# Moving both operands of the large matmuls to equal offsets, and norming two token tiles at a time, in a hybrid encoder layer on one core

## The chip, the core and the metric

The kernel runs on one core of a Trainium2 chip. A core has five engines that each take their instructions in order: TensorE (PE in the profile: matmuls and transposes; its weight loads stand as PEld), VectorE (DVE), ScalarE (ACT), GpSimd (POOL) and SyncE (SP, which issues most loads). They wait for one another through semaphores. Operands lie in SBUF, products in the eight banks of PSUM. The metric is the time of one execution on the device in microseconds; less is better.

## The reference

One layer over 512 tokens of width 2048 in float32: four token mixers that share one input projection, cross-attention to 256 memory tokens, and a gated feed-forward network. Each of the three has a norm before it and one behind it.

```python
def rmsnorm(x, g):
    xf = x.astype(jnp.float32)
    y = xf * lax.rsqrt(jnp.mean(xf * xf, axis=-1, keepdims=True) + EPS)
    return (y * g.astype(jnp.float32)).astype(x.dtype)

def swiglu_ffn(h, w_gu, w_down):
    gate, up = jnp.split(h @ w_gu, 2, axis=-1)
    return (jax.nn.silu(gate) * up) @ w_down

def reference(x, mem, norm_g, w_in, ...):
        u = rmsnorm(x, g[MIX_PRE]) @ w_in[l]
        u_a, u_b, u_c, u_d = jnp.split(u, IN_SPLITS, axis=-1)
        mixed = jnp.concatenate([
            short_conv_mixer(u_a, ...), multiscale_pool_mixer(u_b, ...),
            gated_deltanet_mixer(u_c, ...), mamba2_mixer(u_d, ...)], axis=-1)
        x = x + rmsnorm(mixed @ w_out[l], g[MIX_POST])
        xa = memory_cross_attention(rmsnorm(x, g[XA_PRE]), rmsnorm(mem, g[MEM_NORM]), ...)
        x = x + rmsnorm(xa, g[XA_POST])
        x = x + rmsnorm(swiglu_ffn(rmsnorm(x, g[FFN_PRE]), w_gu, w_down), g[FFN_POST])
```

`ffn_w_gu` is 2048 by 11264 and `ffn_w_down` 5632 by 2048.

## The kernel before

**Products.** TensorE multiplies in a reduced float format (fp32r), so each float32 operand is split into a high and a low part: ACT casts the high part (L149, L152, L962), VectorE subtracts it to get the low one (L150, L153, L963). `mul3` (L167 to L170) makes one product of three matmuls: high by high (L168), high by low (L169), low by high (L170). The first operand that a row names behind the arrow is the moving one, the second the one whose 128 columns are loaded.

**Large projections.** `proj_a` and `proj_b` run over pieces of a weight matrix of 256 by 512 (1,024 numbers a partition); each piece is loaded on SP, split into `whi` and `wlo`, and multiplied with all token tiles: matmuls of 512 columns. The pool `wp` has three buffers of each. `act` holds the activations of a stage, eight buffers; `pt` holds the attention's probabilities, `at_v` the values, for `value_out` (L871). The pools are laid out one behind the other in SBUF; a small pool `padp` on the right and a tile `pad` in `gp` shift what follows.

**Stages.** K projection (to about 115 us), input projection with the gated delta rule and the other mixers (to 750), V projection (to 1000), output projection with the first norm (`advance`), `value_out`, query projection and attention (to 1325), attention's output projection `y_proj` with `vw_d` (1325 to 1421), the second norm, gate and up projection (1478 to 2367), down projection (2375 to 2762), last step.

**The second norm.** `phase2` hands `y_proj` a list of steps (L921): column block 0 for all four token tiles, blocks 1 to 3 for tiles 0 and 1, then blocks 1 to 3 for tiles 2 and 3. After block 3 of a pair, `then` calls `advance_t` (L925) for it. For one tile after the other it loads the residual `x1_d`, forms the reciprocal root of the mean square (`mean_rsqrt`, twelve small instructions on VectorE), adds (L938), stores `x2_d`, norms again (squares on ACT, a second chain), scales on ACT (L941), transposes on TensorE (L946, sixteen) and evicts on VectorE (L948) into `xT`. For tiles 0 and 1 the factors L1 and L2 are split at once. Before the norm of tiles 2 and 3, `begin` (L1051) starts blocks 0 and 1 of the next stage.

**Gate and up projection.** 44 blocks; each computes a 2-by-2 block product with seven products in place of eight (the Winograd form of Strassen's scheme). Product m multiplies the left factor Lm (from `xT`, made once by `left_parts`, L965) with a right factor made from four weight quarters (`right_parts`, L988); it is 24 matmuls of 256 columns. `ORDER` (L959) is the order of the products. Products 1 and 2 go to their own half banks A and B; `gate_first` (L1041) copies A on ACT, adds B on VectorE and forms the gate. Product 6 adds to A, 5 and 3 to Cc, 7 and 4 to A. ACT copies 6 to `f_y` (L1087) before product 7 may write A again.

**Down projection.** Ten panels with the same seven products, 512 columns each, factors B1 to B7 from the hidden activations; `panel` (L1145) loads the four quarters B11, B12, B21, B22 in this order, 1 MB each, and splits them with `factor` (L1171).

**What sets the order.** The code is written per stage; a scheduler moves independent instructions past one another before the program is fixed, so that, for instance, 11 matmuls of product 3 stand ahead of product 7. [...]

Of the kernel before, what the change touches and what calls it, by code (L numbers as in the profile page):

```python
# [7 lines left out]
F32 = mybir.dt.float32  # L8
# [53 lines left out]
def build(tc, x, mem, norm_g, w_in, conv_a_w, pool_w, pool_scale, gdn_conv_w, gdn_A_log,  # L62
# [13 lines left out]
    es_act, es_ps, es_wp, es_stg, es_early = (ExitStack() for _ in range(5))  # L76
    wp = pool("wp", 3, stack=es_wp)

    pool("padp", side="right").tile([P, 8], F32, name="pad")
# [647 lines left out]
    def y_proj(act, W, g, yp, steps):  # L727
# [5 lines left out]
        ss = yp.tile([P, NT, 4], F32, name="yss")  # L733
# [29 lines left out]
    def phase1():  # L763
# [16 lines left out]
        with s1:  # L780
            with ExitStack() as s2:
# [6 lines left out]
                gp.tile([P, 8], F32, name="pad")  # L788
# [97 lines left out]
    def phase2(act):  # L886
        with ExitStack() as s0:
# [22 lines left out]
            def then(i):  # L910
                def f(y, ss):
                    if i == 1:
                        for j in range(2):
                            begun[j] = begin(j, L, ep)
                    advance_t((2 * i, 2 * i + 1), y, ss, xT, pl2)
                    if i == 0:
                        for sub in range(2):
                            split3(L[1][sub], xT[0][0][sub])
                            split3(L[2][sub], xT[1][0][sub])
                return f  # L920
# [4 lines left out]
    def advance_t(tiles, y, ss, xT, pl):  # L925


        for t in tiles:
            rows = slice(t * P, (t + 1) * P)
            xt = pl.tile([P, D], F32, name="ad_x", bufs=2)  # L930
            nc.sync.dma_start(xt, x1_d[rows])
            s = sm.tile([P, 1], F32, name="rs_s")
            nc.vector.tensor_reduce(s, ss[:, t], axis=AX.X, op=ALU.add)
            r = sm.tile([P, 1], F32, name="rs_r")
            mean_rsqrt(r, s, 1, D)
            for q in range(4):
                qs = slice(q * 512, (q + 1) * 512)
                nc.vector.scalar_tensor_tensor(xt[:, qs], y[:, t, qs], r, xt[:, qs], op0=ALU.mult, op1=ALU.add)  # L938
            nc.gpsimd.dma_start(x2_d[rows], xt)
            n = norm_rows(xt, pl)  # L940
            nc.scalar.activation(xt, xt, AF.Copy, scale=n)  # L941
            for q in range(4):
                tp = ps.tile([P, 4, P], F32, name="ps")
                for j in range(4):
                    k = q * 4 + j
                    nc.tensor.transpose(tp[:, j], xt[:, k * P:(k + 1) * P], ident)  # L946
# [12 lines left out]
    ORDER = (1, 2, 5, 6, 7, 3, 4)  # L959
# [5 lines left out]
    def left_parts(A11, A12, A21, A22, tmp, L, given=()):  # L965
# [3 lines left out]
        for m, a in ((1, A11), (2, A12)):  # L969
# [18 lines left out]
    def right_parts(B11, B12, B21, B22, new, begun=False):  # L988

        tt = nc.vector.tensor_tensor  # L990
        if not begun:
            yield B11
            yield B21
# [11 lines left out]
    def gate_up(xT, L, begun):  # L1005

        with ExitStack() as s0:
# [14 lines left out]
            tp = pool("tp", 2, "right", s0, reuse_waits="tile")  # L1022
            for j in range(HT):
# [14 lines left out]
    def half_bank():  # L1038
        return mm.tile([P, 512], F32, name="mm")[:, 0:256]

    def gate_first(A, B, pl):  # L1041

        g, th = pl.tile([P, 256], F32, name="f_g"), pl.tile([P, 256], F32, name="f_t")
        X = pl.tile([P, 256], F32, name="f_x", bufs=1)
        nc.scalar.copy(X, A)
        nc.vector.tensor_tensor(g, B, X, op=ALU.add)
        nc.scalar.activation(th, g, AF.Tanh, scale=0.5)
        nc.vector.scalar_tensor_tensor(g, th, 1.0, g, op0=ALU.add, op1=ALU.mult)
        return g

    def begin(j, L, pl):  # L1051

        A, B = half_bank(), half_bank()
        for m, bank in ((1, A), (2, B)):
            b = wp.tile([P, 8, P], F32, name="raw")
            nc.sync.dma_start(b, w_gu[j, m - 1, 0])
            product(bank, split_w(b), L, m)
        return A, gate_first(A, B, pl)

    def block(j, L, rp, tp, begun):  # L1060
# [7 lines left out]
        parts = right_parts(*q, lambda: tp.tile([P, 8, P], F32, name="sum"), bool(begun))  # L1068
        if begun:
            A, g = begun  # L1070
        else:
            A, B = half_bank(), half_bank()
            for m, bank in ((1, A), (2, B)):
# [246 lines left out]
```

## Time and profile before

| | us |
|---|---|
| median of three runs | 2833.37 (2831.52 to 2834.23) |
| the profiled execution | 2830.88 |
| its span in the profile | 2829.1 |
| TensorE busy | 2736.0 |
| VectorE busy | 1863.6 |
| ACT busy | 1226.0 |
| y_proj's end to the first L5 matmul | 56.6 |
| last matmul of gate_up to the first of the down projection | 8.3 |

The profile shows one execution. Busy time counts an engine's own instructions; a matmul's end is modelled, so consecutive matmuls overlap in the rows, and the pace is read from the distance of their starts. An idle time is named with what ended it.

### The profile page before, as it was taken

How to read it: one execution, taken by the hardware profiler on the slowest of the kernel's cores; microseconds unless marked ns; L12 is line 12 of the kernel's file. 1: busy time of each engine (PE TensorE's matmuls, PEld its weight loads, DVE VectorE, ACT ScalarE, POOL GpSimd, SP SyncE). 2: the span in 40 equal slices, each digit the busy share in tenths (PEclk: the TensorE clock that was granted, in tenths of full speed). 3: DMA queues.
4: the chain of work that ended last, by engine and by line, in shares of the span. 5: the costliest groups of instructions: out<-in, count | busy, mean ns of one | idle time of the engine just before them, and what ended most of it. 6: DMA issues, size and time to landing. Idle time of an engine off the chain costs nothing. (4 is left out here: it accounts for less than half of the span.)

```text
span 2829.1 us, 39953 instructions
## 1 busy us (share of the span) xinstructions
PE 2736.0 (97%) x15890; PEld 2380.0 (84%) x15890; DVE 1863.6 (66%) x2743; ACT 1226.0 (43%) x1866; POOL 115.4 (4%) x175
## 2 busy tenths in 40 slices
PE   8999999999999999999949999999999998999997
PEld 6778788878788877888749999999999997888885
DVE  5735557455752364433787777777777778999976
ACT  5623433233552254432544444444444444555542
POOL 0000001100000001000000000000000000000002
PEclk9999999999999999999979999999999999999998
DMA  8633322334675267433633333333333335567656
GB/s 286 232 100 89 91 71 79 112 119 144 206 268 184 92 237 261 157 100 122 209 119 123 123 113 120 116 116 117 116 116 116 120 113 210 200 185 201 168 141 220
DMA packets 160725, 425.23 MB, mean 150 GB/s; under 512 B 18061, under 2 KB 29210, under 8 KB 149658
## 3 DMA queue, kind: packets, MB, share of 16 engines
q1 hardware_dynamic: 145626, 363.96, 38.9%
q0 software_dynamic: 14912, 58.73, 7.6%
q8 instruction: 124, 2.03, 0.3%
q14 instruction: 63, 0.52, 0.1%
HBM read 348.16 MB, written 74.47 MB: 149 GB/s over the span
## 5 line engine op out<-in xcount | busy, mean ns | idle before, releaser
L153 DVE SCALAR_TENSOR_TENSOR wlo<-raw,PA,whi 128x512 fp32r<-128x512 f32 x368 | 263.5, 748 | 313.5 <-ACT whi L152 313.3
L152 ACT ACTIVATE whi<-raw,PA 128x512 fp32r<-128x512 f32 x368 | 248.0, 718 | 415.2 <-PE mm L169 222.8
L168 PE MATMUL mm<-act,whi 128*128 128x512 f32 x832 | 334.4, 402 | 0.0
L170 PE MATMUL mm<-act,wlo 128*128 128x512 f32 x832 | 331.2, 398 | 0.0
L169 PE MATMUL mm<-act,whi 128*128 128x512 f32 x832 | 330.7, 398 | 0.0
L962 ACT CAST whi<-raw 128x1024 fp32r<-128x1024 f32 x176 | 184.7, 1050 | 279.6 <-PE mm L169 270.4
L963 DVE TENSOR_TENSOR wlo<-raw,whi 128x1024 fp32r<-128x1024 f32 x176 | 215.4, 1225 | 79.9 <-ACT whi L962 79.7
L168 PE MATMUL mm<-whi,act 128*128 128x512 f32 x640 | 255.0, 399 | 2.3 <-ACT act L149 2.3
L169 PE MATMUL mm<-wlo,act 128*128 128x512 f32 x640 | 254.4, 398 | 1.6 <-DVE wlo L153 1.6
L170 PE MATMUL mm<-whi,act 128*128 128x512 f32 x640 | 253.6, 397 | 0.2 <-DVE act L150 0.2
L150 DVE TENSOR_TENSOR wlo<-raw,whi 128x1024 fp32r<-128x1024 f32 x92 | 112.6, 1225 | 195.4 <-ACT whi L149 195.3
L962 ACT CAST whi<-sum 128x1024 fp32r<-128x1024 f32 x132 | 138.5, 1050 | 219.1 <-PE mm L169 211.6
L963 DVE TENSOR_TENSOR wlo<-sum,whi 128x1024 fp32r<-128x1024 f32 x132 | 161.5, 1223 | 79.4 <-ACT whi L962 79.2
L170 PEld LDWEIGHTS mm<-act,wlo 128*128 128x128 f32 x832 | 156.8, 188 | 36.2 <-issue 0.5
L169 PEld LDWEIGHTS mm<-act,whi 128*128 128x128 f32 x832 | 157.1, 189 | 35.0 <-issue 0.7
L168 PEld LDWEIGHTS mm<-act,whi 128*128 128x128 f32 x832 | 157.1, 189 | 34.9 <-issue 0.7
L149 ACT CAST whi<-raw 128x1024 fp32r<-128x1024 f32 x92 | 96.6, 1051 | 191.7 <-PE mm L170 141.1
L168 PEld LDWEIGHTS mm<-whi,act 128*128 128x128 f32 x640 | 120.9, 189 | 31.6 <-ACT act L149 4.2
L169 PEld LDWEIGHTS mm<-wlo,act 128*128 128x128 f32 x640 | 121.0, 189 | 30.1 <-DVE wlo L153 2.9
L170 PEld LDWEIGHTS mm<-whi,act 128*128 128x128 f32 x640 | 121.0, 189 | 27.9 <-DVE act L150 0.6
L168 PE MATMUL mm<-L5h,whi 128*128 128x256 f32 x352 | 100.6, 286 | 23.4 <-ACT whi L962 23.4
L962 ACT CAST whB<-rawB 128x1024 fp32r<-128x1024 f32 x80 | 83.8, 1052 | 53.0 <-PE mm L170 46.9
(539 smaller groups left out, 7262.8 us busy)
## 6 DMA issues: line engine op xcount, KB each, us to landing
raw<-in_w_gu_dram SPq DMA_DIRECT2D x180, 512.0 KB, 3.7
raw<-in_w_in_dram SPq DMA_DIRECT2D x88, 512.0 KB, 3.6
rawB<-in_w_down_dram SPq DMA_DIRECT2D x40, 1024.0 KB, 6.8
raw<-in_xa_wkv_dram SPq DMA_DIRECT2D x64, 512.0 KB, 4.7
raw<-in_w_out_dram SPq DMA_DIRECT2D x32, 512.0 KB, 3.7
raw<-in_xa_wo_dram SPq DMA_DIRECT2D x32, 512.0 KB, 6.3
raw<-in_xa_wq_dram SPq DMA_DIRECT2D x32, 512.0 KB, 3.8
raw<-vw_d SPq DMA_DIRECT2D x28, 512.0 KB, 4.4
```

Source lines behind the costliest of these rows:

```text
L149: nc.scalar.copy(hi, src)
L150: nc.vector.tensor_tensor(lo, src, hi.bitcast(F32), op=ALU.subtract)
L152: nc.scalar.activation(hi, src, AF.Copy, scale=scale)
L153: nc.vector.scalar_tensor_tensor(lo, src, scale, hi.bitcast(F32), op0=ALU.mult, op1=ALU.subtract)
L168: nc.tensor.matmul(o, ah, bh, start=start, stop=False, skip_group_check=reopen)
L169: nc.tensor.matmul(o, ah, bl, start=False, stop=False, skip_group_check=reopen)
L170: nc.tensor.matmul(o, al, bh, start=False, stop=stop, skip_group_check=reopen)
L962: nc.scalar.copy(hl[0], src)
L963: nc.vector.tensor_tensor(hl[1], src, hl[0].bitcast(F32), op=ALU.subtract)
```

## The change

It has five parts. Pads: a pool `padl` of 32 numbers on the left, `padp` of 104 in place of 8, the `pad` in `gp` of 72 in place of 8, and `yss` as a tile of 128 columns. They shift what follows, so that the weight tiles, `act`, `at_v` in both its pools, L1 and L2, B1 and B2 and the last step's tiles begin 64 bytes past a multiple of 512 bytes; before, `act`, L1, L2, B1, B2 and the last step's tiles began 448 past, `at_v` in the pool `adp` 384. Order of products: 2 before 1, with A and B in the two halves of one bank, ACT copying B; Cc moves to the pool `ps`. Second norm: `advance_t` works on its two tiles together, with one chain of small instructions for both, and scales the second tile on VectorE. Five blocks instead of two are begun before their stage. In a panel the same order, so B21 is split first.

```diff
+    pool("padl").tile([P, 32], F32, name="pad")
     wp = pool("wp", 3, stack=es_wp)
-    pool("padp", side="right").tile([P, 8], F32, name="pad")
+    pool("padp", side="right").tile([P, 104], F32, name="pad")
...
-        ss = yp.tile([P, NT, 4], F32, name="yss")
+        ss = yp.tile([P, 128], F32, name="yss")[:, 0:4 * NT].rearrange("p (t c) -> p t c", c=4)
...
-                gp.tile([P, 8], F32, name="pad")
+                gp.tile([P, 72], F32, name="pad")
...
                 def f(y, ss):
-                    if i == 1:
-                        for j in range(2):
-                            begun[j] = begin(j, L, ep)
                     advance_t((2 * i, 2 * i + 1), y, ss, xT, pl2)
                     if i == 0:
                         for sub in range(2):
                             split3(L[1][sub], xT[0][0][sub])
                             split3(L[2][sub], xT[1][0][sub])
+                    else:
+                        for j in range(3):
+                            begun[j] = begin(j, L, ep)
...
     def advance_t(tiles, y, ss, xT, pl):
+        xs = []
         for t in tiles:
             xt = pl.tile([P, D], F32, name="ad_x", bufs=2)
+            nc.sync.dma_start(xt, x1_d[t * P:(t + 1) * P])
+            xs.append(xt)
+        s = sm.tile([P, 2], F32, name="rs_s")
+        for i, t in enumerate(tiles):
+            nc.vector.tensor_reduce(s[:, i:i + 1], ss[:, t], axis=AX.X, op=ALU.add)
+        r = sm.tile([P, 2], F32, name="rs_r")
+        mean_rsqrt(r, s, 2, D)
+        sq = sm.tile([P, 2, 2], F32, name="nr_q")
+        for i, t in enumerate(tiles):
+            for hf in range(2):
+                qs = slice(hf * 1024, (hf + 1) * 1024)
+                nc.vector.scalar_tensor_tensor(xs[i][:, qs], y[:, t, qs], r[:, i:i + 1], xs[i][:, qs],
+                                               op0=ALU.mult, op1=ALU.add)
+                sumsq(xs[i][:, qs], sq[:, i, hf:hf + 1], pl)
+            nc.gpsimd.dma_start(x2_d[t * P:(t + 1) * P], xs[i])
+        s2 = sm.tile([P, 2], F32, name="nr_s2")
+        nc.vector.tensor_reduce(s2, sq, axis=AX.X, op=ALU.add)
+        n = sm.tile([P, 2], F32, name="nr_r2")
+        mean_rsqrt(n, s2, 2, D)
+        for hf in range(2):
+            qs = slice(hf * 1024, (hf + 1) * 1024)
+            nc.scalar.activation(xs[0][:, qs], xs[0][:, qs], AF.Copy, scale=n[:, 0:1])
+            nc.vector.tensor_scalar(xs[1][:, qs], xs[1][:, qs], n[:, 1:2], None, op0=ALU.mult)
+        for q in (0, 2, 1, 3):
+            for i, t in enumerate(tiles):
                 tp = ps.tile([P, 4, P], F32, name="ps")
...
-    ORDER = (1, 2, 5, 6, 7, 3, 4)
+    ORDER = (2, 1, 5, 6, 7, 3, 4)
...
-        for m, a in ((1, A11), (2, A12)):
+        for m, a in ((2, A12), (1, A11)):
...
+            yield B21
             yield B11
-            yield B21
...
+            for j in range(3, 5):
+                begun[j] = begin(j, L, tp)
             for j in range(HT):
                 block(j, L, rp, tp, begun.get(j))
...
+    def begin(j, L, pl, B11=None, B21=None):
+        bank = mm.tile([P, 512], F32, name="mm")
+        A, B = bank[:, 0:256], bank[:, 256:512]
+        tl = lambda n, bufs: pl.tile([P, 256], F32, name="f_" + n, bufs=bufs)
+        X, g = tl("x", 1), tl("g", 3)
+        for m, o, kh, b in ((2, B, 1, B21), (1, A, 0, B11)):
+            if b is None:
+                b = wp.tile([P, 8, P], F32, name="raw")
+                nc.sync.dma_start(b, w_gu[j, kh, 0])
+            product(o, split_w(b), L, m)
+            if m == 2:
+                nc.scalar.copy(X, B)
+        nc.vector.tensor_tensor(g, A, X, op=ALU.add)
+        nc.scalar.activation(X, g, AF.Tanh, scale=0.5)
+        nc.vector.scalar_tensor_tensor(g, X, 1.0, g, op0=ALU.add, op1=ALU.mult)
+        return A, g
...
-        Cc = half_bank()
+        A, g = begun or begin(j, L, tp, q[0], q[2])
+        Cc = ps.tile([P, 512], F32, name="ps")[:, 0:256]
...
-        ws = {1: factor(), 2: factor()}
+        ws = {m: factor() for m in ORDER[:2]}
...
-            if m == 1:
+            if m == 2:
                 X = new("eX")
-                copy(X, A)
-            elif m == 2:
+                copy(X, B)
+            elif m == 1:
                 for t in range(2):
-                    tt(X[:, t], B[t], X[:, t], op=ALU.add)
+                    tt(X[:, t], A[t], X[:, t], op=ALU.add)
```

How it stands on the engines, at three places. First TensorE in a block of gate_up that was not begun early, before: the end of product 2 and the start of product 5 (what a row waits for stands in brackets).

```order
L168 MATMUL mm<-L2h,whi 128x256
L169 MATMUL mm<-L2l,whi 128x256
L170 MATMUL mm<-L2h,wlo 128x256
L168 MATMUL mm<-L5h,whi 128x256 [waits Activation_49]
L169 MATMUL mm<-L5l,whi 128x256
L170 MATMUL mm<-L5h,wlo 128x256 [waits DVE_49]
L168 MATMUL mm<-L5h,whi 128x256
```

After, the same place: product 2 is through, eleven matmuls of product 5 have been started, and product 1 follows.

```order
L170 MATMUL ps<-L5l,whi 128x256
L171 MATMUL ps<-L5h,wlo 128x256
L169 MATMUL ps<-L5h,whi 128x256
L170 MATMUL ps<-L5l,whi 128x256
L169 MATMUL mm<-L1h,whi 128x256 [waits Activation_49]
L170 MATMUL mm<-L1l,whi 128x256
L171 MATMUL mm<-L1h,wlo 128x256
```

Product 1 used to stand ahead of product 2 and wait for its weights alone; now it stands among the matmuls of product 5, and its first matmul waits for an instruction of ACT.

Second, TensorE at the end of the second norm, before: the last transposes, and L5.

```order
L946 MATMUL ps<-C,ad_x 128x128 x3
L946 MATMUL ps<-C,ad_x 128x128 [waits DVE_49]
L946 MATMUL ps<-C,ad_x 128x128 x3
L168 MATMUL mm<-L5h,whi 128x256 [waits Activation_49]
L169 MATMUL mm<-L5l,whi 128x256 [waits DVE_49]
L168 MATMUL mm<-L6h,whi 128x256 [waits Activation_49]
L170 MATMUL mm<-L5h,wlo 128x256 [waits DVE_49]
```

After, the last transposes:

```order
L960 MATMUL ps<-C,ad_x 128x128 [waits DVE_49]
L960 MATMUL ps<-C,ad_x 128x128 x3
L170 MATMUL mm<-L2l,whi 128x256
L960 MATMUL ps<-C,ad_x 128x128 [waits DVE_49]
L960 MATMUL ps<-C,ad_x 128x128 x3
L169 MATMUL mm<-L1h,whi 128x256 [waits Activation_49]
L170 MATMUL mm<-L1l,whi 128x256
L171 MATMUL mm<-L1h,wlo 128x256
```

The transposes now stand between matmuls of products 2 and 1 of blocks begun early; L5 comes about 90 matmuls further on.

Third, ACT at the entry to the down projection, before (`whB` are high parts of weights, `rawB` a load, `hq` and `tmp` hidden activations):

```order
L962 CAST B5h<-tmp 128x1024 [waits DVE_49]
L962 CAST B7h<-hq 128x1024 [waits DVE_49,Activation_49]
L962 CAST whB<-rawB 128x1024 [waits DMAHW2_49]
L962 CAST whB<-rawB 128x1024 [waits DMAHW4_49]
L962 CAST B6h<-tmp 128x1024 [waits DVE_49]
L962 CAST whB<-rawB 128x1024 [waits DMAHW4_49]
L962 CAST whB<-rawB 128x1024
```

After:

```order
L976 CAST B5h<-tmp 128x1024 [waits DVE_49]
L976 CAST B7h<-hq 128x1024 [waits DVE_49,Activation_49]
L976 CAST B6h<-tmp 128x1024 [waits DVE_49]
L976 CAST B3h<-hq 128x1024 [waits DVE_49]
L976 CAST whB<-rawB 128x1024 [waits DMAHW2_49,DMASW3_49,DMASW1_49]
L976 CAST whB<-rawB 128x1024 [waits Activation_49]
L976 CAST whB<-rawB 128x1024 [waits DMAHW0_49]
```

Two more casts of left factors (B6, B3) now stand ahead of the first cast of weights, which reads another load than before.

## Rows read from the trace of the kernel before

**Rows 1.** The page's first section: busy time of each engine, its share, instructions
```profile
PE 2736.0 (97%) x15890; PEld 2380.0 (84%) x15890; DVE 1863.6 (66%) x2743; ACT 1226.0 (43%) x1866; POOL 115.4 (4%) x175
```

**Rows 2.** TensorE's waits: line, releaser, us in total, times, longest
```profile
PE mm L168 <- ACT whB L962: 8.0, 1, 8.0
```

**Rows 3.** Timeline of TensorE: start, duration, line, operands, [idle before, releaser]
```profile
1401.62 2.10 PE L946 MATMUL ps<-C,ad_x 128*128 128x128 f32 x16 [1.51 <-ACT ad_x L941]
...
1414.74 2.10 PE L946 MATMUL ps<-C,ad_x 128*128 128x128 f32 x16 [1.23 <-ACT ad_x L941]
...
1477.83 0.58 PE L168 MATMUL mm<-L5h,whi 128*128 128x256 f32 x1 [23.43 <-ACT whi L962]
```

**Rows 4.** Timeline of TensorE: ends of two dense stretches
```profile
838.29 0.39 PE L170 MATMUL mm<-whi,act 128*128 128x512 f32 x1
...
1016.31 0.40 PE L168 MATMUL mm<-whi,at_vh 128*128 128x512 f32 x1
...
1329.19 0.39 PE L168 MATMUL mm<-whi,pth 128*128 128x512 f32 x1
...
1399.72 0.39 PE L170 MATMUL mm<-whi,ptl 128*128 128x512 f32 x1
```

**Rows 5.** Groups by line, TensorE, 1086 to 1143, then 1153 to 1165
```profile
L170 PE MATMUL mm<-whi,at_vl 128*128 128x512 f32 x17 | 6.7, 395 | 0.0
...
L170 PE MATMUL mm<-whi,at_vl 128*128 128x512 f32 x18 | 7.0, 389 | 0.0
```

**Rows 6.** Stretches, matmuls reading act: length, PE busy (count), clock, DMA
```profile
0.00:100.00 100.00, 82.83 (x338) 1.00 0.89 304
300.00:560.00 260.00, 192.43 (x741) 1.00 0.29 86
...
750.00:800.00 50.00, 37.07 (x151) 1.00 0.55 173
```

**Rows 7.** Timeline of TensorE: a block, first matmuls of products 1, 5, 3
```profile
1878.45 0.28 PE L168 MATMUL mm<-L1h,whi 128*128 128x256 f32 x1
...
1884.15 0.28 PE L168 MATMUL mm<-L5h,whi 128*128 128x256 f32 x1
...
1889.90 0.28 PE L168 MATMUL mm<-L3h,whi 128*128 128x256 f32 x1
```

**Rows 8.** Timeline of ACT: the copy of product 6 in a block
```profile
1809.48 0.36 ACT L1087 COPY f_y<-mm 128x256 f32<-128x256 f32 x1
```

**Rows 9.** Timeline of TensorE behind that copy
```profile
1809.59 0.28 PE L169 MATMUL mm<-L3l,whi 128*128 128x256 f32 x1
1809.89 0.38 PE L168 MATMUL mm<-L7h,whi 128*128 128x256 f32 x1
1810.12 0.28 PE L169 MATMUL mm<-L7l,whi 128*128 128x256 f32 x1
```

**Rows 10.** Timeline of VectorE: evictions, a split, a root's chain, a gate step
```profile
1415.43 2.48 DVE L948 TENSOR_TENSOR stg<-ps,PA 128x512 f32<-128x512 f32 x4 [1.39 <-PE ps L946]
1417.84 1.22 DVE L963 TENSOR_TENSOR L1l<-stg,L1h 128x1024 fp32r<-128x1024 f32 x1
...
1427.35 0.15 DVE L228 TENSOR_SCALAR mr_v<-rs_s 128x1 f32<-128x1 f32 x1
...
1429.67 0.75 DVE L938 SCALAR_TENSOR_TENSOR ad_x<-y,rs_r,ad_x 128x512 f32<-128x512 f32 x1
...
1431.47 0.42 DVE L1046 TENSOR_TENSOR f_g<-mm,f_x 128x256 f32<-128x256 f32 x1
```

**Rows 11.** The stretch to L5: length, PE, PEld, DVE, ACT, POOL, clock
```profile
1421.20:1477.80 56.60, 19.32 (x129) 18.02 (x128) 48.20 (x98) 23.74 (x27) 1.06 (x2) 0.70 0.29 103
```

**Rows 12.** Line 309: count, duration min/median/max ns, first, last, shape
```profile
L309 DVE TENSOR_SCALAR xt<-xt,nr_r x4: 1287/1288/1291, 84.0 to 108.1; 128x2048 f32<-128x2048 f32 x4
```

**Rows 13.** Timeline of ACT: first and third load of the down projection
```profile
2374.42 1.99 ACT L962 CAST whB<-rawB 128x1024 fp32r<-128x1024 f32 x2 [1.05 <-DMA rawB<-in_w_down_dram]
...
2379.41 2.00 ACT L962 CAST whB<-rawB 128x1024 fp32r<-128x1024 f32 x2 [2.05 <-DMA rawB<-in_w_down_dram]
```

More of the change, by code (lines that the diff above doesn't have):

```diff
@@ L925, in advance_t @@
     def advance_t(tiles, y, ss, xT, pl):
+        xs = []
         for t in tiles:
-            rows = slice(t * P, (t + 1) * P)
             xt = pl.tile([P, D], F32, name="ad_x", bufs=2)
[L931 to L942, printed above, removed]
+            nc.sync.dma_start(xt, x1_d[t * P:(t + 1) * P])
[23 more added lines that the diff above has]
+            for i, t in enumerate(tiles):
                 tp = ps.tile([P, 4, P], F32, name="ps")
@@ L945, in advance_t @@
                     k = q * 4 + j
-                    nc.tensor.transpose(tp[:, j], xt[:, k * P:(k + 1) * P], ident)
+                    nc.tensor.transpose(tp[:, j], xs[i][:, k * P:(k + 1) * P], ident)
                 o = t % 2 * P
@@ L1036, in split_w @@
         return w
[L1038 to L1058, printed above, removed]
+    def begin(j, L, pl, B11=None, B21=None):
[14 more added lines that the diff above has]
+        return A, g
     def block(j, L, rp, tp, begun):
@@ L1067, in block @@
         tl = lambda n, bufs=1: tp.tile([P, 256], F32, name="f_" + n, bufs=bufs)
[L1068 to L1073, printed above, removed]
-                product(bank, split_w(next(parts)), L, m)
-            g = gate_first(A, B, tp)
-        Cc = half_bank()
+        parts = right_parts(*q, lambda: tp.tile([P, 8, P], F32, name="sum"), True)
+        A, g = begun or begin(j, L, tp, q[0], q[2])
+        Cc = ps.tile([P, 512], F32, name="ps")[:, 0:256]
         bank = {6: A, 5: Cc, 7: A, 3: Cc, 4: A}
@@ L1095, in block @@
             else:
-                th = tl("t", 2)
+                th = tl("t")
                 nc.scalar.activation(th, A, AF.Tanh, scale=0.5)
```

## The prediction

> **What bounds the kernel now.** I read the page's first section first: TensorE is busy 2736.0 of 2829.1 us [rows 1], so only two things can move the end: the pace at which TensorE takes its matmuls, and the few places where it stands. For the places I read the table of TensorE's waits. It names the first product of the down projection, 8.0 us [rows 2]; TensorE's timeline shows the transposes of the second norm waiting and the longest wait of all, 23.43 us at 1477.83, before the first product that needs the left factors [rows 3]. For the pace I read the distance of one matmul's start from the next where nothing waits: first and last start of a dense stretch, divided by the matmuls in between.
>
> The pace has two values for the same shape. From 838.29 to 1016.31 lie 766 starts of 512 columns, 232.4 ns each; from 1329.19 to 1399.72 there are 311, 226.8 ns each [rows 4]. In the built program the first stretch reads an `act` tile that begins 448 bytes past a multiple of 512 against a weight tile that begins 64 past one; the second reads `pt` and weights, both 64 past. That the operands' distance decides, and not what they hold, is borne out by one piece of code that runs at either: `value_out` takes 395 ns a matmul with `at_v` 384 past, and 389 ns where the same lines run with `at_v` 64 past [rows 5].
>
> **Part 1, the pads.** After the change both operands of all the large matmuls lie 64 past. By the program 5,376 matmuls of 512 columns go from unequal to equal: 4,416 that read `act`, 288 of `value_out`, 480 with B1 or B2 in the down projection, 192 in the last step. The two rows of spacing differ by 5.6 ns, the rows of `at_v` by 6; I take 5.7, so 5,376 x 5.7 = 30.6 us if TensorE sets the pace everywhere. It does not in the start-up, in the recurrence and around 750 to 800, where loads or other engines' chains pace it; 338 + 741 + 151 = 1,230 `act` matmuls lie there [rows 6], and I credit none of them: 4,146 x 5.7 = **-23.6 us**. Ends: -30.6 (all), and -18 if a quarter of the others is lost behind short interruptions, of which the stretches of rows 4 are free.
>
> The same step costs something at 256 columns. In one block of gate_up the 48 matmuls of products 1 and 2 (unequal) take 1878.45 to 1884.15, 118.8 ns each; the next 48 (products 5 and 6, equal) take 5.75 us, 119.8 ns [rows 7]. 44 blocks x 48 x 1.2 ns (1.0 by this block, rounded up as a median block shows 120.0) = **+2.5 us**, with 0 as the other end.
>
> **Part 2, a wait in every block.** A block now runs product 2 into the upper half of a bank, product 1 into the lower half of the same bank, and ACT copies product 2 in between. The order of after shows what this does: the first matmul of product 1 waits for ACT's copy, and eleven matmuls of product 5 stand ahead of it. Before has this very figure once a block: product 7 waits for the copy of product 6, eleven matmuls of product 3 stand ahead. There ACT's copy starts at 1809.48, takes 0.36 and ends after the eleven are through [rows 8]; TensorE goes on at 1809.89 where 1809.71 was due, and needs 0.23 for the next step where 0.12 is usual [rows 9]. That is 0.18 + 0.11 = 0.29 us. On ACT's queue the new copy stands behind one cast of weights just as that one does, and nobody else is kept. 39 of the 44 blocks run this way (five are begun early): 39 x 0.29 = **+11.3 us**. Ends: 0, if ACT happens to be free when product 2 ends; +17, if half a cast more (some 0.15 us) comes before the copy in each.
>
> By the rows alone the wait could be thought needless, since the two halves are different addresses. [...]
>
> **Part 3, tiles 0 and 1 together.** Inside the last projection the transposes of tile 0 and of tile 1 each waited, 1.51 and 1.23 us [rows 3]. Now 32 transposes come in a row behind 47 more projection matmuls, so these 2.7 us go. What comes instead: VectorE gets eight evictions of 0.62 (2.48 for four), four splits of L1 and L2 at 1.2 (1.14 start to start) and two evictions of y at 0.6, 10.8 us in a block [rows 10], and the split whose low half the next projection matmuls need stands behind it, 1.1 more. TensorE covers 4.2 us of that with the transposes (2 x 2.10, rows 3) and 1.4 with six matmuls that need no low half. New wait 11.9 - 5.6 = 6.3, less 2.7: +3.6, and with a little for ACT's casts ahead of the splits **+4 us**. Ends 0 and +9.
>
> **Part 4, tiles 2 and 3 together, five blocks begun early.** From the projection's end to the first L5 matmul 56.6 us pass, in which TensorE has 96 matmuls of blocks 0 and 1 and 32 transposes; VectorE is busy 48.2 of them, ACT 23.7 [rows 11]. So the chain on VectorE decides when L5 starts, and it has 8.4 us of slack at most. Removed: two of four reciprocal-root chains, 2.3 us each (1427.35 to 1429.67, rows 10), -4.6. Added: the scaling of tile 3, 1.3 by the row of a tensor_scalar over 2048 columns [rows 12] and 0.1 for a second instruction; six splits of weights for blocks 2 to 4 at 1.14, 6.8; six gate steps at about 0.35 start to start (0.42 each, rows 10), 2.1. Net +5.7 us of work against 8.4 of slack, so L5 starts 0 to 5.7 later; I take 3. In return the first two products of blocks 2, 3 and 4, 144 matmuls x 0.119 = 17.1 us, run while TensorE would stand. **-14 us**. Ends -18 (L5 no later, the clock kept up: its mean in the stretch is 0.70 before) and -8 (the three blocks' weights stand behind the left factors on VectorE, and TensorE, which keeps its order, waits for them before L5). Loads for three blocks are issued on SP earlier, 512 KB each, in a stretch whose DMA share is 0.29; that hides them.
>
> **Part 5, the entry to the down projection.** The first factor is now B21, the third of the 1 MB loads, since the loads keep their order. ACT began to cast the first at 2374.42 and the third at 2379.41, each when its load had landed [rows 13]; TensorE, which waited 8.0 us [rows 2], waits 5.0 longer: **+5 us**, ends +2 (the factor after it is then ready) and +6.
>
> Cost nothing: the third product bank moved to the other PSUM pool, fewer buffers for the tanh tile, the squares taken in halves on ACT (the same columns), the loads of x1 issued together.
>
> **Sum.** -23.6 + 2.5 + 11.3 + 4 - 14 + 5 = -14.8. The profiled execution took 2830.9 us, so 2816.1; the median of the runs is 2833.4, 2.5 above it, so **2819 us** (rounded).
>
> **Rivals.** *The equality does not bring the pace.* The slow pace would then belong to what `act` and `at_v` adjoin and not to their distance from the weights; part 1 drops out: -14.8 + 23.6 - 2.5 = +6.3, 2840 us, slower. The kernel turns slower at all once under a quarter of part 1 comes (6.3 of 23.6), and by over 0.2% once next to nothing does. Against it speaks `at_v` [rows 5]; for it that no row shows an `act` tile at 64. [...]
>
> *The early blocks only move the wait.* If VectorE does its queue in order, the weights of blocks 3 and 4 come after the left factors, L5 comes after those products on TensorE, and what is gained on five blocks is waited in front of them: part 4 falls from -14 to 0, giving 2833 us, no change. For it: 48.2 of 56.6 us busy on VectorE; against: at most 5.7 us of work is added there against 17.1 taken from TensorE.
>
> *All of the pace and no wait in the blocks.* If the copy is ready when the eleven matmuls end, and the 1,230 matmuls speed up too: -30.6 + 2.5 + 0 + 4 - 14 + 5 = -33, 2800 us. Against it the same figure costs 0.29 us in each block of before.
>
> **How the numbers follow.** The ends of the terms, combined as independent (root of the sum of squares), reach 15 us below the sum and 11 above; three quarters of that, 2808 to 2827, I call the forecast, 0.64; the moved wait 0.15; the pace without effect 0.08; all of the pace 0.10; the rest, 0.03, is spread. A measurement of this kernel can tell about 0.2%, 5.7 us, from no change: faster is below 2827.7, slower above 2839.1. Faster: 0.64 + 0.10 + 0.02 = 0.76; same: 0.15 + 0.01 = 0.16; slower 0.08. The range runs from 2806, between the forecast and the full gain, to 2833, at the moved wait.
>
> **What would show it.** Part 1: 227 ns between starts in the stretch that had 232.4, and 389 for `at_v` everywhere. Part 2: one more step of about 0.3 us in each block, before product 1, put down to ACT's copy. Part 3: no wait at the transposes, but one of some 6 us at a low product in the projection's last column. Part 4: L5 some 60 us after the projection's end, and blocks 2 to 4 with five products. Part 5: the first down matmul 13 us after the last of gate_up. I am wrong if the pace does not change, or if TensorE stands over 10 us longer between the projection and L5 than worked out.

## The result and the profile after

The changed kernel takes 2818.56 us (median of five runs, 2812.74 to 2820.15) against 2833.37 before: a ratio of 0.9945, 95% interval 0.993 to 0.9959, 14.8 us faster. The forecast was 2819. In the profiles the spans are 2814.2 and 2829.1, 14.9 apart, so the profile of after can be read as it stands, stage by stage.

The page's first section of after, which answers to [rows 1] (busy us, share of the span, instructions):

```profile
PE 2721.0 (97%) x15890; PEld 2384.8 (85%) x15890; DVE 1868.8 (66%) x2693; ACT 1220.6 (43%) x1874; POOL 115.9 (4%) x175
```

TensorE is busy 15 us less in a span that is 15 us shorter: the change made its matmuls faster and left the standing, taken together, about as long. Where it stands now, by the table of TensorE's waits (line, releaser, us in total, times, longest), beside [rows 2, 3]:

```profile
PE mm L171 <- DVE wlo L977: 17.6, 2, 15.2
PE mm L169 <- ACT whB L976: 13.4, 1, 13.4
PE mm L170 <- DVE wlo L151: 5.9, 5, 3.9
```

The 23.43 us before L5 became 15.2 at a low product of a block begun early; the wait for the first down factor went from 8.0 to 13.4; a new one of 3.9 came inside the attention's projection.

**The pace.** TensorE's timeline, ends of the dense stretch of the V projection, as [rows 4]:

```profile
830.39 0.39 PE L171 MATMUL mm<-whi,act 128*128 128x512 f32 x1
...
1004.06 0.39 PE L169 MATMUL mm<-whi,at_vh 128*128 128x512 f32 x1
```

766 steps in 173.67 us, 226.7 ns each, where it took 232.4. The group of `at_v` in the pool where it was unequal, in the form of [rows 5] (count, us, mean ns):

```profile
L171 PE MATMUL mm<-whi,at_vl 128*128 128x512 f32 x8 | 3.1, 390 | 0.0
```

390 ns, where 395 stood.

**A block of gate_up.** TensorE where product 1 now waits, and ACT's timeline at that place, to be read as [rows 9] and [rows 8]:

```profile
1900.60 0.28 PE L170 MATMUL ps<-L5l,whi 128*128 128x256 f32 x1
1900.85 0.38 PE L169 MATMUL mm<-L1h,whi 128*128 128x256 f32 x1
1901.08 0.28 PE L170 MATMUL mm<-L1l,whi 128*128 128x256 f32 x1
```

```profile
1899.48 1.06 ACT L976 CAST whi<-sum 128x1024 fp32r<-128x1024 f32 x1 [1.55 <-PE mm L170]
1900.43 0.37 ACT L1067 COPY f_x<-mm 128x256 f32<-128x256 f32 x1
```

The copy of product 2 (`f_x`) begins behind a cast of weights; the first matmul of product 1 comes 0.25 us after the one ahead of it and the next 0.23 later, where 0.12 is due: 0.13 + 0.10 us more, as forecast in kind.

**The norm of tiles 0 and 1.** TensorE (first the transposes, then the low product) and VectorE:

```profile
1388.71 3.61 PE L960 MATMUL ps<-C,ad_x 128*128 128x128 f32 x16 [2.01 <-ACT ad_x L953]
...
1402.57 0.79 PE L170 MATMUL mm<-wlo,pth 128*128 128x512 f32 x1 [3.92 <-DVE wlo L151]
```

```profile
1391.57 4.08 DVE L962 TENSOR_TENSOR stg<-ps,PA 128x512 f32<-128x512 f32 x6 [0.16 <-PE ps L960]
1395.57 1.22 DVE L977 TENSOR_TENSOR L1l<-stg,L1h 128x1024 fp32r<-128x1024 f32 x1
...
1401.31 3.48 DVE L151 TENSOR_TENSOR wlo<-raw,whi 128x1024 fp32r<-128x1024 f32 x3
```

The granted clock there, in the columns of [rows 6] but for all matmuls:

```profile
1388.71:1392.00 3.29, 3.29 (x16) 0.50 0.44 145
1402.57:1405.70 3.13, 3.13 (x7) 0.50 0.53 188
```

The transposes still wait, 2.01 us, and the first sixteen take 3.61 in place of 2.10 [rows 3]. TensorE had stood 0.81, 0.68 and 2.01 us from 1375.5 on, and was then granted 0.50: a transpose starts every 213 ns, where at 1.00 it takes 109. VectorE's evictions wait for the transposes (0.16 us ahead of the third), not the other way round. Behind the evictions come the four splits of L1 and L2 from 1395.57 on, and only at 1401.31 the low parts that the projection needs. After the 3.92 us of waiting for them the clock is 0.50 again, and seven matmuls take 427 ns each in place of 227.

**Tiles 2 and 3, blocks begun early.** TensorE at the low product of block 3 and at L5, and VectorE ahead of it:

```profile
1458.39 0.58 PE L171 MATMUL mm<-L2h,wlo 128*128 128x256 f32 x1 [15.16 <-DVE wlo L977]
...
1469.01 0.28 PE L169 MATMUL ps<-L5h,whi 128*128 128x256 f32 x1
```

```profile
1454.85 2.35 DVE L977 TENSOR_TENSOR L4l<-stg,L4h 128x1024 fp32r<-128x1024 f32 x2
1457.12 3.48 DVE L977 TENSOR_TENSOR wlo<-raw,whi 128x1024 fp32r<-128x1024 f32 x3
```

VectorE splits the last left factor (L4) and only then the weights of block 3. L5 follows 57.3 us after the projection's last matmul (1411.69), 56.8 before.

**Entry to the down projection.** TensorE and ACT, beside [rows 13]:

```profile
2363.62 1.22 PE L169 MATMUL mm<-whB,B2h 128*128 128x512 f32 x2 [13.40 <-ACT whB L976]
```

```profile
2359.77 1.04 ACT L976 CAST B3h<-hq 128x1024 fp32r<-128x1024 f32 x1 [0.21 <-DVE hq L996]
2362.52 3.89 ACT L976 CAST whB<-rawB 128x1024 fp32r<-128x1024 f32 x4 [1.70 <-DMA rawB<-in_w_down_dram]
```

ACT is ready at 2360.8 and stands until the third load lands. The first matmul comes 13.7 us after gate_up's last; before it was 8.3.

The stages of the two traces side by side, from matmul to matmul of the same number (a minus is a gain):

| stretch | before, us | after, us | difference | forecast |
|---|---|---|---|---|
| start to the attention's projection | 1324.8 | 1307.2 | -17.6 | -19.8 |
| inside it, the 96th low product to its end | 29.0 | 37.2 | +8.2 | +4 |
| its end to the end of the fifth block | 151.7 | 134.5 | -17.2 | -14 |
| the other 39 blocks | 794.5 | 803.7 | +9.3 | +13.5 |
| entry to the down projection, first panel | 48.8 | 54.3 | +5.5 | +4.7 |
| the other panels, the last step, the end | | | -3.2 | -3.6 |

From the first to the 96th low product of the attention's projection both take 67.2 us. The forecasts in the first and last line are part 1 split by its counts of matmuls; the fourth line has part 2 and 39 blocks' share of the 256-column loss.

### The profile page after: what moved, and what is told of

The parts are those of the page before. It is cut to its first block, busy times and chain, and to the rows that moved or that the text cites. A ratio compares the mean times of both kernels' runs of the same rounds, so it can differ in the third digit from the quotient of the medians.

```text
span 2814.2 us, 39887 instructions
## 1 busy us (share of the span) xinstructions
PE 2721.0 (97%) x15890; PEld 2384.8 (85%) x15890; DVE 1868.8 (66%) x2693; ACT 1220.6 (43%) x1874; POOL 115.9 (4%) x175
## 5 line engine op out<-in xcount | busy, mean ns | idle before, releaser
L169 PE MATMUL mm<-act,whi 128*128 128x512 f32 x832 | 330.4, 397 | 0.0
L170 PE MATMUL mm<-act,whi 128*128 128x512 f32 x832 | 326.8, 393 | 0.0
L169 PE MATMUL mm<-whi,act 128*128 128x512 f32 x640 | 252.2, 395 | 1.9 <-ACT act L150 1.9
L171 PE MATMUL mm<-whi,act 128*128 128x512 f32 x640 | 250.5, 392 | 0.2 <-DVE act L151 0.2
L171 PE MATMUL mm<-L2h,wlo 128*128 128x256 f32 x352 | 101.1, 288 | 17.6 <-DVE wlo L977 17.6
```

Source lines behind the costliest of these rows:

```text
L169: nc.tensor.matmul(o, ah, bh, start=start, stop=False, skip_group_check=reopen)
L170: nc.tensor.matmul(o, ah, bl, start=False, stop=False, skip_group_check=reopen)
L171: nc.tensor.matmul(o, al, bh, start=False, stop=stop, skip_group_check=reopen)
```

## The experiments

All kernels below ran beside runs of the kernel before on the same chip; medians are theirs. The kernel before itself took 2833.37 us beside after, 2831.50 beside the kernels of offsets alone, offsets undone, own bank and B21 first, 2832.00 beside those of 32 and 256 bytes, the first pair tile by tile and two blocks begun, 2830.73 beside the three parts mended and the left factors 32 bytes off, and 2831.11 beside the last two. So two kernels are compared by how far each lies from the kernel before beside it; after lies 14.8 us under it. A stretch of a trace tells less than a microsecond, medians of four runs some three: the kernels with equal offsets, whose code is the same up to there, reach the first low product of the attention's projection anywhere from 1302.5 to 1308.8 us (the three with unequal ones, before among them, at 1323.9 to 1324.8). So small parts are read from stretches.

### Offsets alone

```diff
-    pool("padp", side="right").tile([P, 8], F32, name="pad")
+    pool("padp", side="right").tile([P, 104], F32, name="pad")
...
-        ss = yp.tile([P, NT, 4], F32, name="yss")
+        ss = yp.tile([P, 128], F32, name="yss")[:, 0:4 * NT].rearrange("p (t c) -> p t c", c=4)
...
-                gp.tile([P, 8], F32, name="pad")
+                gp.tile([P, 72], F32, name="pad")
...
-                th = tl("t", 2)
+                th = tl("t")
```

> The kernel before with the equal offsets alone: every large matmul's two operands lie 64 bytes past a multiple of 512, order of products, norm and early blocks as before (one buffer less for the tanh tile, to make room). Theory (the offsets set the pace): what the trace of after gained up to the end of attention, 17.6 us, comes again, and 3 us behind gate_up; products 1 and 2 lose about 1 ns a matmul, 44 x 48 of them, 2 us: -18.5 us, about 2815. Starts of 512-column matmuls 227 ns apart everywhere. Rival (the pace came with something else in the change, such as the new order or other buffers): 2833, 232 ns.

2814.29 us (2812.12 to 2816.53), ratio 0.9942 (0.9925 to 0.9958). TensorE's timeline, the same dense stretch:

```profile
826.99 0.39 PE L170 MATMUL mm<-whi,act 128*128 128x512 f32 x1
...
1000.66 0.39 PE L168 MATMUL mm<-whi,at_vh 128*128 128x512 f32 x1
```

766 steps of 226.7 ns. The pace is the offsets' doing, and they alone give 17.2 us by the medians and 18.8 by the spans of the traces (2810.3 against 2829.1): as much as the whole change or a little more, by no more than medians tell. So the other parts together bring nothing that these runs can show. In gate_up its 39 blocks behind the fifth take 797.7 us against 794.5: the 256-column loss, +2.2 forecast for them, +3.2 found.

### After with the offsets undone

```diff
-    pool("padp", side="right").tile([P, 104], F32, name="pad")
+    pool("padp", side="right").tile([P, 136], F32, name="pad")
...
-                gp.tile([P, 72], F32, name="pad")
+                gp.tile([P, 8], F32, name="pad")
```

> After, with the pad on the right at 136 and the one in gp at 8, so that act, L1, L2, B1, B2 and the last step's tiles lie again 128 bytes off the weights' place within 512, at_v 256 off; all else as in after. Theory (offsets): +18.5 us against after, about 2837, 232 ns in the stretch of the V projection and 118.8 in products 1 and 2. Rival: 2818.6 as after.

2838.18 us (2832.83 to 2842.93), ratio 1.0024 (1.0013 to 1.0034): 6.7 us slower than before, and so 21.5 worse than after. The same stretch:

```profile
836.23 0.39 PE L171 MATMUL mm<-whi,act 128*128 128x512 f32 x1
...
1014.18 0.39 PE L169 MATMUL mm<-whi,at_vh 128*128 128x512 f32 x1
```

232.3 ns. Without the pace the rest of the change loses; this is the number that the first rival named (2840), had the offsets done nothing. One thing went another way than written: `at_v` stayed at 227.4 ns between starts where nothing waits (233.3 in before); it lay 256 bytes off, and in the next section 256 bytes off gave `act` 226.7, as 0 did.

### How far off

```diff
-    pool("padp", side="right").tile([P, 104], F32, name="pad")
+    pool("padp", side="right").tile([P, 96], F32, name="pad")
```

> After, with the pad on the right 8 numbers smaller: act, L1, L2, B1, B2 and the last step's tiles lie 32 bytes off the weights' place within 512, in place of 0; at_v stays equal. Theory (equal offsets are wanted): 232 ns between starts in the V projection, 118.8 in products 1 and 2, about 2836. Rival (only far distances cost): 227 ns, 2818.

One run, 2836.21 us. The dense stretch, then the first matmuls of products 2 and 5 in a block:

```profile
837.75 0.39 PE L171 MATMUL mm<-whi,act 128*128 128x512 f32 x1
...
1016.46 0.39 PE L169 MATMUL mm<-whi,at_vh 128*128 128x512 f32 x1
...
1893.26 0.28 PE L169 MATMUL mm<-L2h,whi 128*128 128x256 f32 x1
...
1896.09 0.28 PE L169 MATMUL ps<-L5h,whi 128*128 128x256 f32 x1
```

233.3 ns for 512 columns, 0.9 more than with 128 bytes off; and product 2's 24 matmuls take 2.83 us, 117.9 ns each, against 120.0 in after and 118.8 expected.

And with 256 bytes:

```diff
-    pool("padp", side="right").tile([P, 104], F32, name="pad")
+    pool("padp", side="right").tile([P, 40], F32, name="pad")
```

> After, with the pad on the right 64 numbers smaller: the same tiles lie 256 bytes off. Theory (equal offsets within 512 are wanted): 232 ns, about 2836. Rival (what counts is the place within 256 bytes): 227 ns, 2818. Second rival (the cost grows with the distance): above 233 ns.

One run, 2817.22 us, and

```profile
827.35 0.39 PE L171 MATMUL mm<-whi,act 128*128 128x512 f32 x1
...
1001.01 0.39 PE L169 MATMUL mm<-whi,at_vh 128*128 128x512 f32 x1
```

226.7 ns: 256 bytes off is as good as none. So of the distances run in this stretch (226.7 ns at 0 and 256 bytes, 232.3 at 128, 233.3 at 32) the place within 256 bytes tells the paces apart, not the one within 512 as front and forecast had it; every offset of before (384 and 320 bytes between the operands) is unequal by either count, which is why nothing there told them apart.

The same traces answer one question more and leave one. In the V projection the weights are the moving operand and `act` is loaded; behind `value_out` (1171.70 to 1216.26 us in before) `act` is the moving one. There 191 steps without a wait take 233.3 ns each in before and with 32 bytes, 226.7 in after and with 256. So at 512 columns a shifted operand cost time here whether it was the loaded one (5.6 ns at 128 bytes, 6.6 at 32) or the moving one (6.6 at both). But the weights begin 64 bytes past in every kernel here, and only the other operand was shifted: that its distance from the weights counts, and not its own place within 256 bytes, is not shown.

### A bank of its own for product 2

```diff
-        A, B = bank[:, 0:256], bank[:, 256:512]
+        A, B = bank[:, 0:256], ps.tile([P, 512], F32, name="ps")[:, 0:256]
```

> After, with product 2 in a bank of its own (pool ps) in place of the upper half of product 1's bank. Theory (the shared bank makes product 1 wait for ACT's copy): the step of 0.13 and 0.10 us before product 1 goes in 39 blocks, 0.235 x 39 = 9.2 us, about 2809.5; a block takes 20.37 us in place of 20.60. Rival (the copy is waited for anyway, or the three banks of ps now hold up the next block): 2818 to 2820, block 20.6.

2806.62 us (2806.51 to 2808.42), ratio to before 0.9913 (0.9899 to 0.9928): 24.9 us under before, 10.1 better than after. First matmul of product 2 in two blocks running:

```profile
1892.21 0.28 PE L169 MATMUL ps<-L2h,whi 128*128 128x256 f32 x1
...
1912.61 0.28 PE L169 MATMUL ps<-L2h,whi 128*128 128x256 f32 x1
```

20.40 here, 20.38 on average over 38 blocks (774.57 us), where after has 20.61 (783.14): -8.6 us, 9.2 x 38 / 39 = 9.0 expected. In this program product 1 waits for its own weights alone, and the order is 2, 1, 5 with no matmuls of 5 in between. The shared bank made the wait. It is a wait of the program, at a semaphore; whether the chip would have needed it, no run tried.

### B21 loaded first

```diff
-                b = lb.tile([P, 4, 512], F32, name="rawB", bufs=6)
-                nc.sync.dma_start(b, w_down[c, n, kh, f])
-                q.append(b)
+                q.append(lb.tile([P, 4, 512], F32, name="rawB", bufs=6))
+        for i in (2, 0, 1, 3):
+            nc.sync.dma_start(q[i], w_down[c, n, i // 2, i % 2])
```

> After, with the four loads of a down panel issued in the order B21, B11, B12, B22. Theory (the first down factor waits for the third load): the first cast of weights comes 7.2 us after gate_up as in before, not 12.6: -5.4 us, about 2813. Rival (left factors on ACT and VectorE hold it): about 2817, the cast 10 to 11 us after gate_up.

2810.89 us (2807.86 to 2813.82): 20.6 under before, 5.8 better than after. ACT's first cast of down weights:

```profile
2353.19 1.99 ACT L976 CAST whB<-rawB 128x1024 fp32r<-128x1024 f32 x2 [0.80 <-DMA rawB<-in_w_down_dram]
```

7.0 us behind gate_up's end (2346.24), as expected; the first down matmul comes after 8.0 in place of 13.7 us: -5.6, as the medians have it.

### Tiles 0 and 1 one after the other

`advance_1` is the `advance_t` of before, word for word.

```diff
-                    advance_t((2 * i, 2 * i + 1), y, ss, xT, pl2)
+                    (advance_t if i else advance_1)((2 * i, 2 * i + 1), y, ss, xT, pl2)
```

> After, with the second norm of tiles 0 and 1 done one tile after the other as in before (tiles 2 and 3 together as in after). Theory (the 32 transposes in a row put eight evictions and four splits ahead of the low parts that the projection needs): the 8.2 us that the trace of after lost there come back, about 2810.5. Rival (the loss came from the chain for two tiles being longer, and is repaid in the next stretch): 2818 to 2820.

2813.01 us (2810.31 to 2815.20): 19.0 under before, 4.2 better than after. In the projection the whole loss is gone: its last part takes 29.1 us in place of 37.2, -8.2 as expected. But from there to L5 it takes 64.1 in place of 57.3, so only 1.4 us stay. TensorE's timeline has the place:

```profile
1452.18 0.58 PE L171 MATMUL mm<-L2h,wlo 128*128 128x256 f32 x1 [16.36 <-DVE wlo L1003]
```

The low product of block 3 waits 16.36 us, longer than the 15.16 of after. The rival was right that most of the loss is repaid in the next stretch. VectorE's busy time in the two stretches together is 79.5 us in after and 80.0 here; from the projection's end to L5 it is busy 3.7 us more (55.4 against 51.7) and idle 3.0 more. So rather more than half of the 6.7 us that L5 comes later is work of VectorE that is owed anyway and only paid in another place; what made the idle part was not tried.

### Two blocks begun early

```diff
-                        for j in range(3):
+                        for j in range(2):
                             begun[j] = begin(j, L, ep)
...
-            for j in range(3, 5):
-                begun[j] = begin(j, L, tp)
```

> After, with two blocks begun early in place of five. Each of the other three takes 20.6 us again in place of 14.7: +17.7. Theory (VectorE's queue sets L5): its work for three blocks (8.9 us) and the 10 us in which TensorE did blocks 3 and 4 ahead of L5 go, so that L5 comes 13 us sooner; net +5 us, about 2823. Rival (the early blocks ran in time that is idle anyway, L5 comes no sooner): +17.7, 2836.

2824.04 us (2820.66 to 2827.77): 8.0 under before, 6.8 worse than after. TensorE's timeline at L5:

```profile
1456.48 0.58 PE L169 MATMUL ps<-L5h,whi 128*128 128x256 f32 x1 [24.12 <-ACT whi L976]
```

L5 comes 47.4 us after the projection's end, 9.9 sooner than with five blocks. From the 96th low product to the end of the sixth block (number 5) this kernel takes 199.4 us, after 192.3. So three more blocks begun early bring 7.1 us: of the 17.7 that they take out of the blocks, 10 go into a later L5. That is more than half of what the rival of the moved wait claimed.

### Both pairs one tile after the other

```diff
-    pool("padl").tile([P, 32], F32, name="pad")
...
-                    advance_t((2 * i, 2 * i + 1), y, ss, xT, pl2)
+                    advance_1((2 * i, 2 * i + 1), y, ss, xT, pl2)
```

> After, with both pairs of tiles normed one tile after the other as in before, five blocks begun early as in after (the pad on the left goes with it, since smaller tiles lie ahead of the weights; the offsets stay equal). From the projection's start of its fourth column's last part (its 96th low product) to the end of block 5 of gate_up, after takes 192.3 us and e5_tile_by_tile 190.9. Theory (VectorE sets L5): two chains of 2.3 us more there, 1.4 of scaling less, so about 3 us more than e5, 194, and 2816. Rival (with five blocks begun early the chains lie beside other work): 191, 2813. Second rival (the transposes wait for ACT's scaling in front of the begun products, as they did in before): above 198, 2821.

2815.80 us (2814.42 to 2817.89): 15.3 under before, 0.5 better than after. The same stretch takes 193.4 us, 2.5 more than with only the first pair so (190.9): the norm of the last two tiles together is worth 2.5 us. But not by an earlier L5, as was expected: L5 comes 63.6 us after the projection's end here and 64.1 there. The loss lies behind it, 80.2 against 77.2 us to the end of the fifth block: TensorE waited 2.9 us ahead of L5, and from 1466.3 to 1473.1 the granted clock is 0.50, with 213 ns between matmuls in place of 120; in the other kernel it is 1.00 all through. The long wait ahead of L5 is there too, put down to ACT's copy now, which stands behind ACT's casts of left factors, themselves waiting for VectorE (3.50 us at the longest):

```profile
1454.45 0.58 PE L168 MATMUL mm<-L1h,whi 128*128 128x256 f32 x1 [16.53 <-ACT f_x L1092]
```

### Three parts mended

The edits of three sections above in one kernel:

```diff
+        A, B = bank[:, 0:256], ps.tile([P, 512], F32, name="ps")[:, 0:256]
...
+        for i in (2, 0, 1, 3):
+            nc.sync.dma_start(q[i], w_down[c, n, i // 2, i % 2])
...
+                    (advance_t if i else advance_1)((2 * i, 2 * i + 1), y, ss, xT, pl2)
```

> After with three parts mended: product 2 in its own bank, the loads of a panel with B21 first, tiles 0 and 1 one after the other. By the stretches of the three traces they bring 8.6 us (38 blocks of 20.38 in place of 20.61), 5.6 us (entry to the down projection) and 1.5 us (from the projection's last column to L5, where tile by tile gained 8.2 and gave 6.7 back): 2818.6 - 15.7 = 2803. Rival (the differences of the medians add, 12.0 + 7.7 + 5.6): 2793. Second rival (they share one cover and do not add): above 2806.

2800.36 us (2795.87 to 2803.91), ratio 0.9892 (0.9876 to 0.9909). Product 2 in two blocks running:

```profile
1887.00 0.28 PE L169 MATMUL ps<-L2h,whi 128*128 128x256 f32 x1
...
1907.39 0.28 PE L169 MATMUL ps<-L2h,whi 128*128 128x256 f32 x1
```

By the stretches 2803 was expected, by the medians' sum 2793. It is 30.4 us under before and so 15.6 better than after, where the stretches gave 15.7.

### Left factors 32 bytes off

The second tile of `yss` is cut to 16 numbers to make room.

```diff
+        ss = yp.tile([P, 128 if g == 1 else 16], F32, name="yss")[:, 0:4 * NT].rearrange("p (t c) -> p t c", c=4)
...
+            ep.tile([P, 8], F32, name="pad", bufs=1)
...
             lp = pool("lp", 2, stack=s0, reuse_waits="tile")
+            lp.tile([P, 8], F32, name="pad", bufs=1)
```

> The kernel of e9_three_mended, with a pad of 8 numbers behind L1 and L2 and one ahead of L3 to L7, so that all left factors of gate_up lie 32 bytes off the weights' place; all 512-column operands stay equal. Theory (at 256 columns unequal offsets are the faster ones: with 32 bytes off, products 1 and 2 ran 2.1 ns a matmul faster than with 0): 168 x 2.1 = 0.35 us a block, 20.03 in place of 20.38, 15.5 us in 44 blocks, about 2787. Rival (that gain is eaten by the waits for splits and copies): 20.3 us a block, 2800.

2780.81 us (2777.67 to 2784.37), ratio 0.982 (0.9805 to 0.9834): the fastest kernel of this study, 49.9 us under before, where the changed one is 14.8 under. Product 2 in two blocks running:

```profile
1902.75 0.28 PE L169 MATMUL ps<-L2h,whi 128*128 128x256 f32 x1
...
1922.77 0.28 PE L169 MATMUL ps<-L2h,whi 128*128 128x256 f32 x1
```

20.02 here, 19.99 on the mean. The gain was 0.40 a block, where 0.35 was expected. With four times the distance:

```diff
-            ep.tile([P, 8], F32, name="pad", bufs=1)
+            ep.tile([P, 32], F32, name="pad", bufs=1)
...
-            lp.tile([P, 8], F32, name="pad", bufs=1)
+            lp.tile([P, 32], F32, name="pad", bufs=1)
```

> The kernel of e10_left_factors_off_32, with 128 bytes in place of 32 between the left factors' place and the weights'. Theory (at 256 columns the gain depends on the distance: 1.2 ns at 128 in the trace of before, some 3 at 32): 168 x 1.2 = 0.2 us a block under that of e9_three_mended, 20.18, about 2791. Rival (any distance will do): 19.99 us a block, 2781.

2790.49 us (2789.52 to 2795.44), 40.6 under before:

```profile
1887.39 0.28 PE L169 MATMUL ps<-L2h,whi 128*128 128x256 f32 x1
...
1907.56 0.28 PE L169 MATMUL ps<-L2h,whi 128*128 128x256 f32 x1
```

20.17 here, 20.21 on the mean: the distance matters at 256 columns, 32 bytes gain 3 ns a matmul and 128 gain 1.2 (product 5: 116.9, 118.8 and 120.0 ns at 32, 128 and 0). With 32 bytes products 1 and 2 gain less, 118.3 and 118.1 ns; why was not tried.

## Why the prediction was right, point by point

The time was forecast within half a microsecond, which is more than the steps earned: part 1's gain and part 2's loss were set too high, part 3's loss and part 4's gain too low, and these balanced.

**Part 1** was right in mechanism and nearly in size: 21.1 us by the table (17.6 + 3.2, and 0.3 in the first panel) against 23.6. By the two kernels that add or undo it it is 17 to 21.5, the loss at 256 columns already taken off, against 21.1. The choice not to credit the start-up, the recurrence and the stretch around 750 was sound: between the matmuls at 317 and 538 us, where the recurrence runs, the lead did not grow (4.4 and 4.5 us). What was lost besides were the short interruptions named as the lower end. The rival that had the pace depend on something else is gone: the pace of one and the same stretch changes with the address of one operand alone (226.7, 232.3 and 233.3 ns at 0, 128 and 32 bytes between them).

**Part 2** was right in its place, too dear in its size: 0.235 us a wait, not 0.29. The figure of before was taken over exactly, but the wait that it was taken from also changed, from 0.29 to 0.235: product 7 follows product 3 after 1.45 us in after and after 1.51 in the kernel with offsets alone. So 39 blocks lost 9.3 us, not 13.5 with the 256-column part. It is the shared bank, as the kernel with two banks shows (20.38 us a block in place of 20.61). The two different addresses did not make the wait go: the program waits at a semaphore although the halves do not overlap. Whether the chip needs that wait, no run here shows.

**Part 3** failed in two steps. The 2.7 us of waiting at the transposes did not go: they still waited 2.0, and not 32 came in a row but 16, then 4, 4 and 8 between matmuls. And the sum has no term for the clock, which before held at 1.00 through this stretch and after fell to 0.50 twice: the sixteen transposes and the seven matmuls cost 2.9 us more by that. The low product waited 3.9, where 6.3 had been worked out; two waits ahead of the transposes, 0.8 and 0.7, are new. Together this made 8.2 and not 4.

**Part 4** was right in mechanism and too low in its gain, 17.2 and not 14. L5 came 0.5 us later and not 3, but 24 matmuls of the early blocks, 2.9 us, stand behind the first L5 matmul, so that the step of 3 was sound. What the sum left out lies behind L5: in before 25 matmuls there start some 213 ns apart, at a granted clock of 0.50 to 1484.8, and in after none, which is 2.3 of the missing 3.2 us; its named waits behind L5 are 1.3 us in sum before and 0.8 after. Nor does the stretch stand alone: part of what VectorE does for tiles 0 and 1 in the projection it need not do behind it. Parts 3 and 4 together were forecast at -10 and came to -9.0. By the experiments 7.1 of it are the early blocks beyond two, 2.5 the norm of the last tiles together, and the first pair together costs 1.4. The rival of the moved wait was given 0.15; its mechanism is real, 10 of 17.7 us, only not the whole.

**Part 5** was right: 5.4 us at the first matmul against 5, and taken away by loading in the order of use.

## What to carry to other kernels

Before the order of work is touched, read the distance of matmul starts where nothing waits; if one shape has two paces, compare the addresses of both operands modulo 256, and measure each width by itself, for 512 columns here wanted equal places (226.7 ns against 233.3 with 32 bytes) and 256 columns wanted them 32 bytes apart (116.9 against 120.0). If two products share a PSUM bank, look whether the program makes one wait for a copy of the other: here product 1 waited for the copy out of the other half, 0.235 us a block, and with a second bank that wait was gone. Where an engine's queue sets the end of a stretch, work moved out of it on that engine can come back in the next (here more than half of 6.7 us); take both stretches together before calling either a gain. Where a stretch takes longer than its waits explain, look at the granted clock: here a wait of 3.92 us cost twice, once while TensorE stood and once in the seven matmuls behind it, which took 427 ns each at a clock of 0.50 in place of 227.

## What the runs showed of the hardware that was not expected

- With 512 columns a matmul started every 226.7 ns when both operands lay at the same place within 256 bytes (0 and 256 bytes between them), every 232.3 with 128 bytes between them, every 233.3 with 32 or 64 (the last is `at_v` of before). These are for a shifted loaded operand; a shifted moving one took 233.3 both at 128 and at 32.
- With 256 columns, where the moving operand was shifted, it was the other way round: 120.0, 118.8 and 116.9 ns at 0, 128 and 32 bytes (product 5). At 512 columns a shifted moving operand was slower (233.3 against 226.7 ns), so the sign turned with the width and not with which operand was shifted; why was not tried.
- Behind waits of 0.8, 0.7 and 2.0 us, and again behind one of 3.9, TensorE was granted 0.50 in place of 1.00: transposes took 213 ns in place of 109, matmuls of 512 columns 427 in place of 227. Before, behind waits of 1.5 and 1.2, it stayed at 1.00.
- The wait of product 7 for ACT's copy became 0.06 us shorter when product 3's bank moved to another pool (1.51 to 1.45 us); both runs of the copy stand behind a cast of the same length. What makes it is open.
